# A two-layer decoder kernel: both heads of a pair step together in the attention of both layers, layer 0's memory rows of w_o are used whole, and x's first tiles and squares move at the start

## The chip, the cores and the metric

The program runs on one core of a Trainium2 chip. The metric is the device time of one execution in microseconds, the median of several runs. The core has a matrix engine (PE, also called TensorE), VectorE (DVE), ScalarE (ACT), GpSimd (POOL) and SyncE (SP), which issues most of the DMAs. Each engine works through its own instructions in order and waits on semaphores for the others.

## The reference

The input x is 256 positions by 1024, the memory another 256 by 1024, all in float32. What is computed, cut to what matters here:

```
for layer in (0, 1):
    if layer == 1: shared_kv = moba_kv(h)              # keys and values of 12 heads, once
    h = h + 0.5 * swiglu(rms_norm(h, ffn1_g[layer]))   # "a" in layer 0, "c" in layer 1
    hn = rms_norm(h, mix_g[layer])
    if layer == 0:
        u = hn @ a_w_in;  q_mem = u[..., 2 * CONV_CH:]
        primary = silu(layer_norm(conv31(a * sigmoid(gate)) + bias))   # causal, depthwise, 768 channels
    else:
        u = hn @ b_w_in;  q_mem = u[..., 768:]
        primary = causal_attention(rope(rms_norm(q)), shared_kv)       # 12 heads of 64, own block of 256
    logits = einsum('bshd,bmhd->bhsm', q_mem, k_mem)                   # 4 heads of 64, 256 memory rows
    mem_out = softmax(logits) @ v_mem
    h = h + concatenate([primary, mem_out]) @ w_o[layer]               # 768 + 256 rows
    h = h + 0.5 * swiglu(rms_norm(h, ffn2_g[layer]))   # "b" in layer 0, "d" in layer 1
```

## The kernel before

Activations stand transposed: 128 of the 1024 model channels on the partitions, the 256 positions along the free axis, so a tile of x is one of eight 128x256 pieces, k = 0 to 7. All weights are streamed from memory by SP in chunks of 1 MB (tile "raw", three buffers). Each half of a chunk is split into a high part wh, rounded by ACT (L174), and a low part wl = raw - wh, subtracted by DVE (L176). A product takes three matmuls of reduced-precision floats, high by high, high by low and low by high (function mm3); the scheduler shows them as `oao<-cat,wh` (two) and `oao<-cat,wl` (one). The activations are split the same way into y or cat (index 0 high, 1 low). Where a matmul takes plain float32 operands instead, the profile shows it as two records.

Attention (attend_pair, L469 to L537) handles a pair of heads, which share one 128-partition tile of q and k, head 0 on partitions 0 to 63 and head 1 on 64 to 127. It gives one generator for each head, with eight steps: the scores S; the row minima nb (the scores are negated) on DVE; the exponentials on ACT, with the row sums; reciprocal and scaling on DVE; the transposes of the probabilities into pp on PE; the copy pT of pp to SBUF, by ACT for head 0 and by DVE for head 1; the product with v into o; and, once for both heads, the split of o into cat by ACT and DVE. In a causal head the mask is added by an extra bfloat16 matmul of 128 columns behind each of the two score matmuls. `go(head, n)` runs the next n steps of a generator, and so the order of the calls sets the order on each engine. In layer 1 ("ab0" to "ab5" are the causal pairs, "am10" and "am11" the memory pairs) a loop over the 16 heads does, for head h: scaling and transposes of h, scores of h+2, exponentials of h+2 and so on; the row "order" PVA makes PE, DVE and ACT keep to that order.

In layer 0 the convolution has 31 taps for 768 channels. Five of its six channel groups are done by PE and DVE; parts of them and of the last go as multiply on ACT (cq, L712) and add on POOL (L713), the last group's POOL chain being the longest. Then come the layer norm over channels (mean lnm, subtraction, squares L766, sums lnv, the variance lnvc, the power lnr on POOL, its broadcast lnb), Silu, and the split into cat. The memory attention of layer 0 ("am00", "am01") runs beside it. The output projection ("oao" in layer 0, "obo" in layer 1) starts with the memory rows k = 6 and 7, whose cat comes first, and then takes k = 0 to 5 for each of the eight output tiles m. In layer 0 the low parts of the first four halves of w_o are subtracted by POOL (L180), each behind a POOL instruction named in `lo_after`.

At the start raw0's first quarter is the first DMA on SP, and x's tiles come on the ACT and SP queues. The squares of x are made by ACT and summed by seven adds on POOL (L258) into aacc, from which the first RMS norm comes (anrp on PE).

Of the kernel before, what the change touches and what calls it, by code (L numbers as in the profile page):

```python
# [17 lines left out]
P = 128  # L18
DM = 1024
KD = DM // P  # L20
SEQ = 256
# [27 lines left out]
LO_POOL = 4  # L49
TURN_AT = 3  # L50
# [28 lines left out]
def tile_kernel(ctx: ExitStack, tc: tile.TileContext, w, xT, memT, pos, vec, hg, const, out):  # L79
# [43 lines left out]
    state = {"chunk": 0, "half": 0, "raw": None, "order": "", "last": {}}  # L123
# [40 lines left out]
    def half_chunk(lo_after=None):  # L164
# [7 lines left out]
        for c in range(0, HC, q):  # L172
            s = slice(c, c + q)
            state["act"] = nc.scalar.activation(wh[:, s], raw[:, s], AF.Copy)  # L174
            if lo_after is None:
                state["dve"] = nc.vector.tensor_tensor(wl[:, s], raw[:, s], wh[:, s].bitcast(F32), op=ALU.subtract)  # L176
        if lo_after is None:
            pass
        else:
            behind(nc.gpsimd.tensor_tensor(wl, raw, wh.bitcast(F32), op=ALU.subtract), lo_after)  # L180
# [3 lines left out]
    def tiles_of(n_half, n_lo=0, lo_after=None):  # L184
        for n in range(n_half):
            wh, wl = half_chunk(lo_after[n] if n < n_lo else None)
            for i in range(8):
                yield wh[:, i * P:(i + 1) * P], wl[:, i * P:(i + 1) * P]
# [109 lines left out]
    def ffn(name, y, acc, nexts, store=False, both=False, hook=None, after=None):  # L298
# [3 lines left out]
        for j in range(KF):  # L302
# [4 lines left out]
            if first and j == 0:  # L307
# [161 lines left out]
    def attend_pair(name, qT, kT, v, vcol0, pair, cat, kc, causal, third=-1):  # L469

        po = {}

        def steps(e):
            hs = slice(e * HD, (e + 1) * HD)
            S = psum(f"{name}s{e}", *(("mm", 4) if e == third else ("sc", 2)))
            if causal:
                spans = ((0, P), (P, 3 * P))
                width = 3 * P
            else:
                spans = ((0, SEQ), (SEQ, 2 * SEQ))  # L480
                width = 2 * SEQ
            for t, (lo, hi) in enumerate(spans):
                mmul(S[:, lo:hi], qT[hs, pair, t * P:(t + 1) * P], kT[hs, pair, :hi - lo],
                     start=True, stop=not causal)
                if causal:
                    mmul(S[:, hi - P:hi], identb, maskb, start=False, stop=True)
            yield

            nb = tp.tile([P, NT], F32, name=f"{name}n{e}", tag="nb", bufs=4)
            if causal:  # L490
                for t, (lo, hi) in enumerate(spans):
                    in_order("V", nc.vector.tensor_reduce(nb[:, t:t + 1], S[:, lo:hi], axis=AX.X, op=ALU.min))
            else:
                in_order("V", nc.vector.tensor_reduce(nb, S.rearrange("p (t k) -> p t k", t=NT), axis=AX.X,
                                                      op=ALU.min))
            yield
            pr = tp.tile([P, 512], F32, name=f"{name}p{e}", tag="pr", bufs=4)
            sm = tp.tile([P, NT], F32, name=f"{name}u{e}", tag="sm", bufs=4)
            for t, (lo, hi) in enumerate(spans):
                state["func"] = in_order("A", nc.scalar.activation(  # L500
                    pr[:, lo:hi], S[:, lo:hi], AF.Exp, bias=nb[:, t:t + 1], scale=-1.0, accum_out=sm[:, t:t + 1]))
            yield
            rs = tp.tile([P, NT], F32, name=f"{name}rs{e}", tag="rs", bufs=4)
            in_order("V", nc.vector.reciprocal(rs, sm))
            for t, (lo, hi) in enumerate(spans):
                in_order("V", nc.vector.tensor_scalar(pr[:, lo:hi], pr[:, lo:hi], rs[:, t:t + 1], None, op0=ALU.mult))
            yield
            pp = psum(f"{name}pp{e}", "aux", 2)
            if causal:
                blocks = ((0, 0), (P, P), (2 * P, 2 * P))  # L510
            else:
                blocks = ((0, 0), (P, 2 * P), (2 * P, P), (3 * P, 3 * P))
            for src, dst in blocks:
                transp(pp[:, dst:dst + P], pr[:, src:src + P], ident)
            yield
            pT = tp.tile([P, 512], F32, name=f"{name}t{e}", tag="pT")
            if e:
                in_order("V", nc.vector.tensor_copy(pT[:, :width], pp[:, :width]))
            else:
                in_order("A", nc.scalar.activation(pT[:, :width], pp[:, :width], AF.Copy))  # L520
            yield
            if e == 0:
                po[0] = psum(name + "o")
            o = po[0]
            vc = slice(vcol0 + e * HD, vcol0 + (e + 1) * HD)
            mmul(o[hs, :SEQ], v[:, 0, vc], pT[:, :SEQ], start=True, stop=False)
            if causal:
                mmul(o[hs, P:SEQ], v[:, 1, vc], pT[:, SEQ:SEQ + P], start=False, stop=True)
            else:
                mmul(o[hs, :SEQ], v[:, 1, vc], pT[:, SEQ:], start=False, stop=True)  # L530
            yield
            if e:
# [456 lines left out]
```

## Time and profile before

| | us |
|---|---|
| median of 3 runs | 1023.68 |
| the runs lie between | 1020.43 and 1024.15 |
| the profiled execution | 1020.23 |
| its span, first to last instruction | 1018.1 |
| PE busy | 1000.8 (98%), 5828 matmuls |
| DVE busy | 749.1 (74%) |
| ACT busy | 592.7 (58%) |
| POOL busy | 151.7 (15%) |

The mean granted clock of PE is 0.993 of full speed. A row of the timeline names the start in us from the span's beginning, the length, the engine, the line, the instruction, output and inputs, the shapes, the number of records merged, and in brackets how long the engine had been idle and what released it. An x4 of a plain float32 product is two matmuls. The ends of matmuls are modelled, so the time that one takes from the others is read from the start of one row to the start of the next.

### The profile page before, as it was taken

Reading aid. Unit: us, or ns where it says so; the run is one execution under the profiler, and the core shown is the slowest. Engines: PE = TensorE matmul, PEld = TensorE weight load, DVE = VectorE, ACT = ScalarE, POOL = GpSimd, SP = SyncE. Lnnn points to the kernel's source line nnn. Section 1 sums busy time; section 2 is a strip of 40 time slices with the busy share of each in tenths; the row PEclk is TensorE's granted clock in tenths of the full one; section 3 lists DMA queues with packets and bytes.
Section 4 is the critical chain, followed back from the end, with each engine's and each line's share of the span. In section 5 each row is a group of like instructions: output and inputs, shape, how many; then the busy total and the mean of one; then the engine's idle time right before and its main releaser. Section 6 shows DMA issues by size and latency. Waiting matters only on the chain.

```text
span 1018.1 us, 15614 instructions
## 1 busy us (share of the span) xinstructions
PE 1000.8 (98%) x5828; PEld 868.4 (85%) x5828; DVE 749.1 (74%) x1332; ACT 592.7 (58%) x1117; POOL 151.7 (15%) x164
## 2 busy tenths in 40 slices
PE   8999999999899999999999999999999999999998
PEld 6888888898679888888888888888995798888887
DVE  7987776769867877767766877767786488777663
ACT  6787665547556655555556765555554465555542
POOL 3310000148812000001131020001150030000000
PEclk9999999999989999999999999999999999999999
DMA  8656455534134655554545455546441046545560
GB/s 302 224 196 207 173 200 182 192 103 146 42 108 146 221 188 201 174 204 171 201 165 205 169 186 187 194 179 205 170 163 42 1 166 207 201 171 202 171 227 22
DMA packets 26427, 173.44 MB, mean 170 GB/s; under 512 B 3184, under 2 KB 4592, under 8 KB 6000
## 3 DMA queue, kind: packets, MB, share of 16 engines
q1 hardware_dynamic: 25776, 171.76, 48.1%
q8 instruction: 45, 0.74, 0.3%
q10 hardware_dynamic: 576, 0.70, 0.2%
q14 instruction: 30, 0.25, 0.1%
HBM read 171.39 MB, written 1.05 MB: 169 GB/s over the span
## 4 chain that ended last, share of the span: by engine, by line
PE 92%; DVE 3%; ACT 2%; POOL 1%; DMA 1%; issue 1%; SPq 0%; DVEq 0%; POOLq 0%; ACTq 0%
PE cg L143 8%; PE dg L143 6%; PE du L143 6%; PE co L143 6%; PE ao L143 6%; PE do L143 6%; PE bo L143 6%; PE bg L143 6%; PE bu L143 6%; PE ag L143 6%; PE au L143 6%; PE cu L143 6%; PE kv L143 3%; PE oao L143 2%; PE mkv L143 2%; PE obo L143 2%
## 5 line engine op out<-in xcount | busy, mean ns | idle before, releaser
L176 DVE TENSOR_TENSOR wl<-raw,wh 128x1024 fp32r<-128x1024 f32 (+1 forms) x309 | 380.1, 1231 | 178.4 <-ACT wh L174 177.8
L174 ACT ACTIVATE wh<-raw 128x1024 fp32r<-128x1024 f32 (+1 forms) x313 | 330.2, 1057 | 303.3 <-PE dg L143 28.4
L143 PE MATMUL ag<-y,wh 128*128 128x512 f32 x176 | 63.6, 396 | 1.8 <-DVE y L249 1.8
L143 PE MATMUL dg<-oby,wh 128*128 128x512 f32 x176 | 63.6, 400 | 0.0
L143 PE MATMUL cg<-by,wh 128*128 128x512 f32 x176 | 62.7, 395 | 0.8 <-DVE cgs L216 0.8
L143 PE MATMUL au<-y,wh 128*128 128x512 f32 x176 | 63.5, 396 | 0.0
L143 PE MATMUL du<-oby,wh 128*128 128x512 f32 x176 | 63.4, 399 | 0.0
L143 PE MATMUL cu<-by,wh 128*128 128x512 f32 x176 | 62.7, 395 | 0.0
L143 PE MATMUL bg<-oay,wh 128*128 128x512 f32 x176 | 62.4, 395 | 0.0
L143 PE MATMUL bu<-oay,wh 128*128 128x512 f32 x176 | 62.2, 394 | 0.0
L143 PE MATMUL co<-chs,wh 128*128 128x512 f32 (+1 forms) x198 | 61.9, 369 | 0.0
L143 PE MATMUL ao<-ahs,wh 128*128 128x512 f32 (+1 forms) x198 | 61.9, 369 | 0.0
L143 PE MATMUL do<-dhs,wh 128*128 128x512 f32 (+1 forms) x198 | 61.9, 369 | 0.0
L143 PE MATMUL bo<-bhs,wh 128*128 128x512 f32 (+1 forms) x198 | 61.9, 368 | 0.0
L143 PE MATMUL ag<-y,wl 128*128 128x256 f32 x176 | 49.9, 284 | 0.3 <-DVE wl L176 0.3
L143 PE MATMUL ao<-ahs,wl 128*128 128x256 f32 x176 | 49.7, 283 | 0.0
L143 PE MATMUL co<-chs,wl 128*128 128x256 f32 x176 | 49.7, 283 | 0.0
L143 PE MATMUL cu<-by,wl 128*128 128x256 f32 x176 | 49.6, 282 | 0.0
L143 PE MATMUL do<-dhs,wl 128*128 128x256 f32 x176 | 49.6, 283 | 0.0
L143 PE MATMUL bo<-bhs,wl 128*128 128x256 f32 x176 | 49.6, 283 | 0.0
L143 PE MATMUL au<-y,wl 128*128 128x256 f32 x176 | 49.5, 282 | 0.0
L143 PE MATMUL cg<-by,wl 128*128 128x256 f32 x176 | 49.4, 281 | 0.0
(983 smaller groups left out, 2519.8 us busy)
## 6 DMA issues: line engine op xcount, KB each, us to landing
raw<-in_w SPq DMA_DIRECT2D x158, 1024.0 KB, 4.8
raw<-in_w SPq DMA_DIRECT2D x5, 512.0 KB, 7.3
mT<-in_memT SPq DMA_DIRECT2D x1, 1024.0 KB, 8.4
out<-x SPq DMA_DIRECT2D x8, 128.0 KB, 2.0
raw<-in_w SPq DMA_DIRECT2D x2, 256.0 KB, 4.2
x<-in_xT ACTq DMA_DIRECT2D x2, 256.0 KB, 5.5
x<-in_xT SPq DMA_DIRECT2D x2, 256.0 KB, 4.8
gt<-in_hg SPq DMA_DIRECT2D x1, 192.0 KB, 4.5
```

Source lines behind the costliest of these rows:

```text
L143: return in_order("P", nc.tensor.matmul(*a, **k))
L174: state["act"] = nc.scalar.activation(wh[:, s], raw[:, s], AF.Copy)
L176: state["dve"] = nc.vector.tensor_tensor(wl[:, s], raw[:, s], wh[:, s].bitcast(F32), op=ALU.subtract)
```

## The change

Four things are changed. Both heads of a pair now go through attend_pair in one generator, and each step does both heads: the score matmuls alternate between head 0 and head 1, as do those with v; one mask matmul of 2x128 columns serves both spans of a head; in causal pairs both copies pT are made by ACT. The loop of layer 1 goes over eight pairs: scale p, scores and minima of p+2, exponentials of p+1, the product with v of p-1, transposes and copies of p.

In layer 0 the memory attention's result is kept whole in float32 (`whole`), and the memory rows of w_o are taken from raw unsplit, two matmul records for each of 16 products instead of three matmuls. POOL subtracts no low parts any more. The rest of w_o is packed so that k = 0 to 3 of all eight m come first, then k = 4 and 5 for each m. Its first four halves are split by ACT and DVE, and `hold` puts these behind the last square and the last mean subtraction of the layer norm. In the convolution's first chunks, the mean of squares stands before the gate's last product, and the broadcast and first gated output stand behind the third product rather than the eighth.

At the start x's first two tiles come first on SP, the others sooner, and the sum of squares is one DVE reduction over eight square tiles in place of seven POOL adds.

```
-LO_POOL = 4
-TURN_AT = 3
+TURN_AT = 2
...
+    nc.sync.dma_start(x[:, :2], xT[:, :2])
     nc.sync.dma_start(raw0[:, :HC // 2], w[0][:, :HC // 2])
-    nc.scalar.dma_start(x[:, :2], xT[:, :2])
+    nc.scalar.dma_start(x[:, 4:6], xT[:, 4:6])
     nc.sync.dma_start(x[:, 2:4], xT[:, 2:4])
     nc.sync.dma_start(raw0[:, HC // 2:HC], w[0][:, HC // 2:HC])
-    nc.scalar.dma_start(x[:, 4:6], xT[:, 4:6])
+    nc.scalar.dma_start(x[:, 6:], xT[:, 6:])
     nc.sync.dma_start(raw0[:, HC:], w[0][:, HC:])
-    nc.sync.dma_start(x[:, 6:], xT[:, 6:])
...
+            state["dve"] = nc.vector.tensor_tensor(wl[:, s], raw[:, s], wh[:, s].bitcast(F32), op=ALU.subtract)
+            if state["hold"]:
+                for i, other in zip((state["act"], state["dve"]), state["hold"]):
+                    behind(i, other)
...
+                sq = cp.tile([P, KD, SEQ], F32, name="sq0", tag="kv")
                 for k in range(KD):
-                    square_sum(f"{name}q0{k}", acc, x[:, k], k == 0)
+                    nc.scalar.activation(sq[:, k], x[:, k], AF.Square)
+                nc.vector.tensor_reduce(acc, sq.rearrange("p k s -> p s k"), axis=AX.X, op=ALU.add)
...
+    def attend_pair(name, qT, kT, v, vcol0, pair, causal, tag, done):
+        hs = [slice(e * HD, (e + 1) * HD) for e in range(2)]
+        S = [psum(f"{name}s{e}", *(("mm", 4) if tag == "mm" else ("sc", 2))) for e in range(2)]
+        spans = ((0, P), (P, 3 * P)) if causal else ((0, SEQ), (SEQ, 2 * SEQ))
+        width = spans[1][1]
+        opened = []
+        for t, (lo, hi) in enumerate(spans):
+            for e in range(2):
+                i = mmul(S[e][:, lo:hi], qT[hs[e], pair, t * P:(t + 1) * P], kT[hs[e], pair, :hi - lo],
+                         start=t == 0 or not causal, stop=not causal, skip_group_check=causal)
+                if t:
+                    behind(i, opened[e])
+                opened.append(i)
+        if causal:
+            for e in range(2):
+                mmul(S[e].rearrange("p (a b) -> p a b", b=2 * P)[:, :, :P], identb,
+                     maskb[:, None, :].to_broadcast([P, 2, P]), start=False, stop=True, skip_group_check=True)
+        yield
...
+        pT = [tp.tile([P, 512], F32, name=f"{name}t{e}", tag="pT") for e in range(2)]
+        in_order("A", nc.scalar.activation(pT[0][:, :width], pp[0][:, :width], AF.Copy))
+        if causal:
+            in_order("A", nc.scalar.activation(pT[1][:, :width], pp[1][:, :width], AF.Copy))
+        else:
+            in_order("V", nc.vector.tensor_copy(pT[1][:, :width], pp[1][:, :width]))
+        yield
+        o = psum(name + "o")
+        vc = [slice(vcol0 + e * HD, vcol0 + (e + 1) * HD) for e in range(2)]
+        for e in range(2):
+            mmul(o[hs[e], :SEQ], v[:, 0, vc[e]], pT[e][:, :SEQ], start=True, stop=False)
+        for e in range(2):
...
+        yield
+        done(o[:, :SEQ])
+        yield
...
+    def to_whole(dst, i):
+        def done(o):
+            state["func"] = in_order("A", nc.scalar.activation(dst[:, i], o, AF.Copy))
+        return done
...
+            start = m % 2 == 0 and k == CC
+            if k >= CC and whole is not None:
+                c = ((k - CC) * KD + m) * P
+                i = mmul(o[m], raw[:, c:c + P], whole[:, k - CC], start=start, stop=False, skip_group_check=True)
+            else:
+                i = mm3(o[m], next(it), cat, k, start, last, skip_group_check=True)
...
+        early = CC - 2 if whole is not None else 0
+        state["hold"] = hold
+        for k in range(early):
+            for m in range(KD):
+                mm(m, k, False)
+        state["hold"] = None
         for m in range(KD):
-            for k in range(CC):
+            for k in range(early, CC):
...
+    whole = hc[:, CC * (PAD + SEQ):CC * (PAD + SEQ) + 2 * SEQ].rearrange("p (i s) -> p i s", i=2)
...
+            mm3(pa[:, :SEQ], wts[0][KD - 1], y[0], KD - 1, False, True)
             v = mean_cols("cnr", acc)
+            mm3(pg[:, :SEQ], wts[1][KD - 1], y[0], KD - 1, False, True)
...
-            mm_group(pa, y[0])
-            rr["b"] = bcast_rows("cnb", rr["r"])
-            glu_out(0, *rr["p"])
+            for k, wt in enumerate(tiles_of(1)):
+                mm3(pa[:, :SEQ], wt, y[0], k, k == 0, k == KD - 1)
+                if k == 2:
+                    rr["b"] = bcast_rows("cnb", rr["r"])
+                    glu_out(0, *rr["p"])
...
+    oproj = out_proj("oa", cat, V_FFN2, whole, (hi, lo))
+    go(pairs[0], 2)
+    go(pairs[1], 4)
+    go(pairs[0], 2)
+    pv = psum("lnv", "mm", 4)
...
     tables(AF.Silu)
+    go(pairs[1], 2)
     with tc.high_priority():
         rlb = bcast_rows("lnb", rl)
-    next(oproj)
-    next(oproj)
+    go(pairs[1], 2)
+    for _ in range(5):
+        next(oproj)
...
+    go(pairs[0], 3)
...
+    n = len(pairs)
+    for p in range(n + 1):
+        if p < n:
+            go(pairs[p], 1)
+        if p == TURN_AT:
             for turn in turns:
                 turn()
+        if p + 2 < n:
+            go(pairs[p + 2], 2)
+        if p + 1 < n:
+            go(pairs[p + 1], 1)
+        if p:
+            go(pairs[p - 1], 2)
+        if p < n:
+            go(pairs[p], 2)
+        if p >= n - 2:
             next(oproj)
...
+        rest = [t[:, :, :early].transpose(0, 2, 1, 3).reshape(P, -1), t[:, :, early:CC].reshape(P, -1)]
+        chunks(np_.concatenate(rest, axis=1))
...
-    out_w(d["w_o"][0])
+    out_w(d["w_o"][0], CC - 2)```

PE in the loop of layer 1, ahead of the scores of the pair ab4; S tiles are ab4s, o tiles ab2o or ab1o, transposed probabilities pp. Before:

```order
L143 MATMUL ab4s_8239<-kvs,q1T 128x128
L143 LDWEIGHTS identb
L143 MATMUL ab4s_8239<-maskb,identb 128x128
L143 MATMUL ab4s_8239<-kvs,q1T 128x256
L143 LDWEIGHTS identb
L143 MATMUL ab4s_8239<-maskb,identb 128x128
L143 MATMUL ab2o<-ab2t_8233,kvs 64x256
L143 MATMUL ab2o<-ab2t_8233,kvs 64x128
L146 MATMUL ab3pp_8255<-cst,ab3p_8210 128x128 x3
```

The nine rows are the work of one head and come twice for a pair. The same place on PE now, where 8143 and 8144 are the S tiles of the two heads:

```order
L142 MATMUL ab4s_8143<-kvs,q1T 128x128
L142 MATMUL ab4s_8144<-kvs,q1T 128x128
L142 MATMUL ab4s_8143<-kvs,q1T 128x256
L142 MATMUL ab4s_8144<-kvs,q1T 128x256
L142 LDWEIGHTS identb
L142 MATMUL ab4s_8143<-maskb,identb 128x2x128
L142 LDWEIGHTS identb
L142 MATMUL ab4s_8144<-maskb,identb 128x2x128
L142 MATMUL ab1o<-ab1t_8131,kvs 64x256
L142 MATMUL ab1o<-ab1t_8132,kvs 64x256
L142 MATMUL ab1o<-ab1t_8131,kvs 64x128
L142 MATMUL ab1o<-ab1t_8132,kvs 64x128
```

Six transposes of ab2 follow. The work of both heads stands side by side, and the product with v is that of the pair before the one whose transposes follow.

ACT in layer 0, from the squares of the layer norm (hc<-hc) to the first Silu (lp), with the second memory pair's exponentials am01p between. Before:

```order
L766 ACTIVATE hc<-hc 128x256 x6
L500 ACTIVATE am01p_2936,am01u_2937<-am01s_2931,am01n_2934 128x256 x2
L500 ACTIVATE am01p_2959,am01u_2960<-am01s_2954,am01n_2957 128x256 x2
L533 ACTIVATE cat_2836<-am00o 128x256
L140 ACT_TABLE_LOAD
L140 ACTIVATE warm<-onec 128x1
L520 ACTIVATE am01t_2992<-am01pp_2987 128x512
L803 ACTIVATE lp_3036<-lz_3034,vt 128x256
```

And now the same stretch:

```order
L799 ACTIVATE hc<-hc 128x256 x6
L173 ACTIVATE wh_0_3062<-raw_3060 128x1024
L173 ACTIVATE wh_1_3090<-raw_3060 128x1024
L173 ACTIVATE wh_0_3120<-raw_3118 128x1024
L173 ACTIVATE wh_1_3148<-raw_3118 128x1024
L504 ACTIVATE am01p_2935,am01u_2937<-am01s_2925,am01n_2931 128x256 x2
L552 ACTIVATE hc<-am00o 128x256
L139 ACT_TABLE_LOAD
L139 ACTIVATE warm<-onec 128x1
L504 ACT_TABLE_LOAD
L504 ACTIVATE am01p_2936,am01u_2938<-am01s_2926,am01n_2932 128x256 x2
L525 ACTIVATE am01t_2985<-am01pp_2975 128x512
```

A third table load and the first Silu follow. Four high parts have come between the squares and the exponentials, and the table is changed three times where it was changed once. On DVE, the first rows behind the minima am01n, up to the layer norm's variance lnvc and the scaling am01p; now:

```order
L497 TENSOR_REDUCE am01n_2932<-am01s_2926 128x2
L174 TENSOR_TENSOR wl_0_3063<-raw_3060,wh_0_3062 128x1024
L174 TENSOR_TENSOR wl_1_3091<-raw_3060,wh_1_3090 128x1024
L174 TENSOR_TENSOR wl_0_3121<-raw_3118,wh_0_3120 128x1024
L174 TENSOR_TENSOR wl_1_3149<-raw_3118,wh_1_3148 128x1024
L812 TENSOR_SCALAR lnvc<-lnv 128x2
```

These four low parts stood on POOL before; they are now ahead of lnvc on DVE.

## Rows read from the trace of the kernel before

**Rows 1.** The page: chain that ended last by engine, and two costly groups.

```profile
PE 92%; DVE 3%; ACT 2%; POOL 1%; DMA 1%; issue 1%; SPq 0%; DVEq 0%; POOLq 0%; ACTq 0%
L176 DVE TENSOR_TENSOR wl<-raw,wh 128x1024 fp32r<-128x1024 f32 (+1 forms) x309 | 380.1, 1231 | 178.4 <-ACT wh L174 177.8
L174 ACT ACTIVATE wh<-raw 128x1024 fp32r<-128x1024 f32 (+1 forms) x313 | 330.2, 1057 | 303.3 <-PE dg L143 28.4
```

**Rows 2.** Windows: stretch, its length, PE, PEld, DVE, ACT, POOL busy, clock, DMA.

```profile
778.61:789.16 10.55, 10.55 (x54) 6.22 (x53) 6.79 (x25) 5.19 (x22) 0.00 (x0) 1.00 0.00 1
...
295.70:299.00 3.30, 3.30 (x18) 3.30 (x17) 1.90 (x3) 2.33 (x5) 0.00 (x0) 0.51 0.00 0
9.00:12.50 3.50, 3.50 (x13) 2.91 (x12) 3.50 (x5) 3.01 (x7) 3.27 (x4) 0.51 0.96 358
```

**Rows 3.** Timeline, PE, from one head of layer 1's loop.

```profile
789.16 0.49 PE L143 MATMUL ab4s<-kvs,q1T 64*128 64x128 f32 x2
...
790.36 0.23 PE L143 MATMUL ab4s<-maskb,identb 128*128 128x128 bf16 x1
790.52 0.86 PE L143 MATMUL ab2o<-ab2t,kvs 128*64 128x256 f32 x4
791.32 0.55 PE L146 MATMUL ab3pp<-cst,ab3p 128*128 128x128 f32 x3
```

**Rows 4.** Timeline, PE: two heads in one stretch, and one head alone.

```profile
291.67 1.09 PE L143 MATMUL am01o<-am01t,mv 128*64 128x256 f32 x8
752.74 1.14 PE L143 MATMUL am10s<-mk,q1T 64*128 64x256 f32 x8
760.19 1.13 PE L143 MATMUL am11s<-mk,q1T 64*128 64x256 f32 x4
```

**Rows 5.** Timeline, ACT: one copy of transposed probabilities in the loop.

```profile
791.96 0.49 ACT L520 ACTIVATE ab3t<-ab3pp 128x384 f32<-128x384 f32 x1 [0.15 <-PE ab3pp L146]
```

**Rows 6.** Timeline, PE: memory pairs and the projection behind the loop.

```profile
767.81 1.08 PE L143 MATMUL am10o<-am10t,mv 128*64 128x256 f32 x4 [0.98 <-DVE am10t L518]
...
799.97 0.40 PE L143 MATMUL obo<-cat,wh 128*128 128x256 f32 x2
...
800.33 0.40 PE L143 MATMUL obo<-cat,wh 128*128 128x256 f32 x2
```

**Rows 7.** Line L713 (POOL's adds of the convolution): idle before it.

```profile
  ACT cq L712: 9.6, 5
```

**Rows 8.** Timeline, layer 0's layer norm and memory attention, all engines.

```profile
273.65 0.62 DVE L506 TENSOR_SCALAR am00p<-am00p,am00rs 128x256 f32<-128x256 f32 x2
...
274.81 7.06 POOL L180 TENSOR_TENSOR wl<-raw,wh 128x1024 fp32r<-128x1024 f32 x3
...
275.36 2.07 PE L143 MATMUL lnm<-hc,onem 128*128 128x256 f32 x4 [4.84 <-DVE hc L724]
275.42 4.24 DVE L506 TENSOR_SCALAR am00p<-am00p,am00rs 128x256 f32<-128x256 f32 x2
...
282.79 2.71 PE L143 MATMUL lnv<-onel,hc 128*128 128x1 f32 x23
...
283.75 0.68 DVE L494 TENSOR_REDUCE am01n<-am01s 128x2 f32<-128x512 f32 x1
...
287.78 1.28 ACT L140 ACT_TABLE_LOAD   x1
...
289.08 0.20 ACT L140 ACTIVATE warm<-onec 128x1 f32<-128x1 f32 x1
...
294.64 0.51 PE L143 MATMUL oao<-cat,wh 128*128 128x256 f32 x2 [1.88 <-DVE cat L534]
```

**Rows 9.** Timeline, the start: first product, a square, a later product.

```profile
8.08 0.50 PE L143 MATMUL ag<-y,wh 128*128 128x512 f32 x1 [1.83 <-DVE y L249]
...
8.66 0.41 ACT L257 ACTIVATE aq<-x 128x256 f32<-128x256 f32 x1
...
13.92 0.39 PE L143 MATMUL ag<-y,wl 128*128 128x256 f32 x1 [0.28 <-DVE wl L176]
```

More of the change, by code (lines that the diff above doesn't have):

```diff
@@ L120, in tile_kernel @@
     nc.vector.memset(mhalf, -0.5)
-    state = {"chunk": 0, "half": 0, "raw": None, "order": "", "last": {}}
+    state = {"chunk": 0, "half": 0, "raw": None, "order": "", "last": {}, "hold": None}
     def behind(i, other):
@@ L467, in queries @@
         return use
[L469 to L489, printed above, removed]
+    def attend_pair(name, qT, kT, v, vcol0, pair, causal, tag, done):
[16 more added lines that the diff above has]
+        yield
+        nb = [tp.tile([P, NT], F32, name=f"{name}n{e}", tag="nb", bufs=4) for e in range(2)]
+        for e in range(2):
@@ L513, in steps @@
[L513 to L524, printed above, removed]
@@ L553, in mem_kv, with out_proj @@
         return kT, v
-    def out_proj(name, cat, g, *lo):
+    def out_proj(name, cat, g, whole=None, hold=None):
         o = []
-        it = tiles_of(KD, *lo)
-        first = {}
+        raw = raw_chunk() if whole is not None else None
+        it = tiles_of(KD if whole is None else KD - 2)
         def mm(m, k, last):
-            i = mm3(o[m], next(it), cat, k, m % 2 == 0 and k == CC, last, skip_group_check=True)
+            start = m % 2 == 0 and k == CC
+            if k >= CC and whole is not None:
+                c = ((k - CC) * KD + m) * P
+                i = mmul(o[m], raw[:, c:c + P], whole[:, k - CC], start=start, stop=False, skip_group_check=True)
+            else:
+                i = mm3(o[m], next(it), cat, k, start, last, skip_group_check=True)
             if k == CC:
-                first[m] = i
                 if m % 2:
-                    behind(i, first[m - 1])
+                    behind(i, state["first"])
+                else:
+                    state["first"] = i
         for m in range(0, KD, 2):
@@ L575, in out_proj @@
             mm(m + 1, CC, False)
+        if whole is not None:
+            yield
         for m in range(KD):
@@ L743, in tile_kernel @@
     cat = y_tiles("cat0")
-    heads = [st for pr_ in range(2)
-             for st in attend_pair(f"am0{pr_}", qT, kT, v, pr_ * P, pr_, cat, CC + pr_, False)]
+    pairs = [attend_pair(f"am0{i}", qT, kT, v, i * P, i, False, "sc", to_whole(whole, i)) for i in range(2)]
     last_conv(22)
@@ L751, in tile_kernel @@
         nc.vector.tensor_tensor(cv[:, CC - 1], last[:, :SEQ], cv[:, CC - 1], op=ALU.add)
-    go(heads[0], 4)
-    go(heads[1], 4)
+    go(pairs[0], 4)
     pm = psum("lnm", "aux", 2)
@@ L805, in tile_kernel @@
         nc.vector.tensor_tensor(cat[:, c, 1], p_, cat[:, c, 0].bitcast(F32), op=ALU.subtract)
-    go(heads[2], 2)
-    go(heads[3], 2)
-    next(oproj)
     state["order"] = ""
@@ L835, in tile_kernel @@
     mq = qT[:, NPAIR:]
[L836 to L842 removed]
+    pairs = [attend_pair(f"am1{i}", mq, kT, v, i * P, i, False, "mm" if i % 2 else "sc", to_cat(cat, CC + i))
+             for i in range(2)]
+    pairs += [attend_pair(f"ab{i}", qT, kTs, vs, i * P, i, True, "mm" if i % 2 else "sc", to_cat(cat, i))
+              for i in range(NPAIR)]
     proj("mq1", y, queries("mq1", re, G_MQ + 1, qT, NPAIR, False, nc.gpsimd))
```

125 lines of the change are left out of this document (43 added, 82 removed).

## The prediction, made before the changed kernel ran

> **What bounds the kernel now.** I read the chain of waits first: 92% of it is PE, with DVE, ACT and POOL at 3% or less each [rows 1]. So a term counts only where PE idles, or where PE's own time shrinks. The windows come next, to see what PE does in the two attention stretches. In the loop of layer 1, 10.55 us for two pairs, PE is busy all the time while DVE is busy 6.79 and ACT 5.19 [rows 2]: PE alone sets the pace there, 5.27 a pair. Then the timeline of one head of that loop, for what PE spends on what [rows 3], and of the few places where two heads' matmuls stand side by side [rows 4]. Last the layer norm of layer 0, where PE does wait: 4.84 us before lnm and 1.88 before oao [rows 8], and the start, where it waits 1.83 [rows 9].
>
> **Layer 1, the loop.** A head before: from the scores at 789.16 to the product with v at 790.52 are 1.36, the two masks in it 790.52 - 790.36 = 0.16 each, so the scores alone are 1.04. The product with v takes 791.32 - 790.52 = 0.80, and the rest of the head's 10.55 / 4 = 2.64, 0.47, is the three transposes [rows 2, 3].
>
> What side by side is worth is in the trace already: eight score records of two heads took 1.14, four of one head 1.13; eight records of products with v took 1.09, four 256 wide in am10o 1.08 [rows 4, 6]. The second head's cost nothing there: each head has 64 of the 128 rows (form 64*128) or columns (128*64). So a pair's scores cost 1.04 and its products with v 0.80. The transposes fill the whole array and stay at 2 x 0.47 = 0.94. A mask of 256 columns has no row; it lies between 0.16 (one mask of 128) and 0.32 (two); I take 0.21, near the lower, since it is the row of the same instruction, so 0.42 for two. Sum 1.04 + 0.42 + 0.80 + 0.94 = 3.20.
>
> The others must keep up. DVE loses one copy of transposed probabilities a pair, which I price like ACT's, 0.49 [rows 5]: 6.79 / 2 - 0.49 = 2.9. ACT gains it: 5.19 / 2 + 0.49 = 3.1 [rows 2, 5]. Both are under 3.20, with little to spare: 0.1 on ACT. In the new order ACT's queue has the exponentials of p+1, then the split of p-1, then the copies of p, and PE has the scores of p+2 to do while the copies run, so no engine waits for the other within a turn unless ACT slips. Six causal pairs save 6 x (5.27 - 3.20) = 12.4. In the two memory pairs the scores of am11 and the products with v of both go side by side; am10's scores already did. At 1.05 for each of the three [rows 4, 6] that is 3.1.
>
> Against it stand new waits at the head of the loop. One wait is there now, 0.98 before am10o [rows 6]. With both heads in one step, PE has less to do while DVE scales two heads, so the first pairs wait longer: between nothing and one turn of DVE, 2.9. I take 1.5. Layer 1: -12.4 - 3.1 + 1.5 = -14.0. Bounds: -15.5 without new waits; with a period of 4.0 in place of 3.20, -9.2.
>
> **Layer 0.** The path to lnm is POOL's chain of adds, which waited 9.6 us in five places for ACT's cq [rows 7]. Now the gated output that opens the chain comes five products sooner: 5 x 0.36 (800.33 - 799.97, [rows 6]) = 1.8. And the high parts of w_o no longer stand among the cq's on ACT; they were two pairs of 1.06 [rows 1]. I take 2.9 of the rest of those waits as gone. Together -4.7, between 0 and -9.6.
>
> Behind lnm, DVE's scaling of am00p took 4.24 beside POOL's subtractions and 0.62 before they began [rows 8]. The mean is copied by DVE behind it, at 275.42 + 4.24 = 279.66, while lnm had ended at 275.36 + 2.07 = 277.43. With no low parts on POOL that 2.2 goes. The wait before oao (1.88) goes too, because PE now has the whole product of k = 0 to 3 behind k = 6 and 7.
>
> What comes in: four high parts on ACT behind the last square and four low parts on DVE behind the first of these, 1.06 + 4 x 1.23 = 6.0 [rows 1], ahead of lnvc on DVE. The sums of squares on PE cover some 2.8 of it (2.71, [rows 8]), which leaves +3.2. This is the cost of the hold: on POOL these subtractions stood beside the path. Then two more table loads on ACT, of 1.28 each [rows 8], one ahead of the second head's exponentials and one ahead of the first Silu. The second is hidden while oao runs, since k = 6 and 7 need no Silu; the first is not: +1.3.
>
> The Trainium skill (ScalarE: Activation LUTs, What ACT_TABLE_LOAD costs) adds about 1.38 us of draining to a load's 1.28. Here the load at 287.78 ends at 289.06 and the next ACT row starts at 289.08 [rows 8], so the trace shows no such drain; by the page both loads together would cost 2.8 more, and the sum would be 1006.9.
>
> Last, the 16 memory products are two plain float32 records each, in place of three matmuls at 0.36. Nothing in the rows shows that record alone with 128 rows; from am01o and am10o, four records of 256 columns in 1.08 [rows 6], it is 0.27 or less, so a product at most 0.54 and at least the 0.36 of the old one. I take the middle, 0.45: 16 x 0.09 = +1.4, between 0 and +2.9. Layer 0: -4.7 - 2.2 - 1.9 + 3.2 + 1.3 + 1.4 = -2.9. Between everything hidden, -6, and nothing gained before lnm, +1.5.
>
> **The start.** ACT has five more squares and one more y ahead of the second quarter of wh, 6 x 0.41 = 2.5, and DVE's one reduction of 2048 elements a partition, at 0.68 for 512 [rows 8, 9], is 2.7, ahead of the second wl: 5.2 of work put before what PE needs for its second k. At most 1.8 of it comes back by x landing first (PE's wait before its first product, [rows 9]). So the product that stood at 13.92 moves by between -1.8 and 5.2 - 1.8 = +3.4. I take the middle, +0.8. The seven POOL adds cost PE nothing before: no row of PE waits for them.
>
> **The sum.** Against the profiled execution's 1020.2: 1020.2 - 14.0 - 2.9 + 0.8 = 1004.1. The median of the runs shown is 3.5 above that execution; I put a quarter of this on top: 1005.
>
> **The rivals.**
>
> ACT becomes the bound of the loop. PE and ACT are 0.1 apart, and each turn has several handovers between them, any of which may open a gap; a period of 4.0 adds 6 x 0.8 = 4.8, so 1009 to 1010. For it: the copies are the last thing in ACT's turn, and both the next transposes and the next product with v wait for them. Against it: PE has scores queued in just that gap. The Trainium skill (TensorEngine Tiling (Array Packing), PSUM Bottleneck) says that side-by-side tiles speed TensorE but not the emptying of PSUM, which may then be the bound. By that rule the pair's time would be ACT's 3.1 or more, which is what this rival prices. No row of before bears on it, as PE set the pace.
>
> Layer 0 and the start lose. If POOL's chain ends no earlier, or the held halves stay whole on the path, layer 0 gives +1.5; with +2.5 at the start the sum is 1020.2 - 14.0 + 4.0 = 1010. For it: the hold puts 6.0 of splitting on the path that POOL used to hide.
>
> Layer 0 gives all its bound, -6: 1020.2 - 14.0 - 6 + 0.8 = 1001, 1002 beside the median.
>
> The heads don't run side by side once they are causal, with scores 128 and 256 wide in one accumulation. Then a pair saves only the masks, 4 x 0.16 - 0.42 = 0.2, and the sum is 1020.2 - 1.3 - 2.9 + 0.8, about 1017. Against it: memory scores did so in the same form [rows 4].
>
> On the other side: the clock. PE's granted clock was at the lower of its two levels (1.2 GHz of 2.4), 0.51 in the rows' scale, from 9.0 to 12.5 behind the idle time of 1.83, and again from 295.7 to 299 behind 1.88 [rows 2, 8, 9]; the 0.98 before am10o cost nothing of it, as the loop ran at 1.00 [rows 2, 6]. If new waits of two us and more come at the head of the loop, and gaps in each turn keep it low, PE's 3.20 becomes 6.4. It decides from the share of the loop at the low level: at 65% a pair takes 5.27 again. In the whole loop it is 6 x 1.1 = +6.8 and, with the memory pairs likewise, about +10: 1020.2 + 10 - 2.9 + 0.8 = 1028, and 1029 beside the median. Against it: PE would still be busy nearly all the time, as 3.20 of work a turn leaves no idle time.
>
> **How the numbers follow.** Chances: my forecast 0.61, with its own range of 1000.5 to 1009; ACT as the bound 0.15; layer 0 and the start losing 0.12; all of layer 0's bound 0.05; heads not side by side 0.03; the low clock 0.04. The range must reach both 1010s and some way past, and down to layer 0's bound with no new waits: 999.5 to 1012. A measurement of this kernel tells some 0.5%, about 5 us, from no change. From the median that puts the limit at 1018.6; the first four cases are all below it. Heads apart and half of the low clock lie within 0.5%, the rest is slower; with something for what I have not thought of, 0.93, 0.04 and 0.03.
>
> **What would show it.** The loop right: the scores of ab3, ab4 and ab5 start 3.2 to 3.4 us apart, and obo ends some 14 us sooner against the first memory scores. Wrong: 4 us apart, with PE waiting for ACT's copies. Layer 0 right: lnm without a wait, low parts on DVE between the squares and lnvc, no wait between k = 6 and k = 3 of oao. Wrong: idle time of PE before am01o or lnb. The start right: a wait of PE for the reduction at about 13 us and the next k within 1 us of before. My prediction is wrong as a whole if the six causal pairs together save less than 8 us.

## The result, and the profile after

The changed kernel took 1012.15 us (median; 1011.14 to 1012.63), beside 1022.94 for the kernel before on the same chip: a ratio of 0.9896, 95% interval 0.9875 to 0.9918. It is faster by 10.8 us, where 18 were forecast, and lies just above the range's upper end of 1012. Its profiled execution took 1012.62 us, with a span of 1010.5.

Four landmarks split the difference, each the first matmul of a stage: mkv, the products with the memory's keys and values; bo, the last product of layer 0's second feed-forward part (part b); am10s, layer 1's first memory scores; and dg, the last feed-forward part. The timeline's summary by tile gives form, count, shortest, median and longest duration in ns, and the first and last start in us. Of the kernel before:

```profile
L143 PE MATMUL mkv<-wh,my x64: 387/389/403, 61.4 to 599.6; 128*128 128x512 f32 x64
L143 PE MATMUL bo<-bhs,wh x198: 274/396/400, 439.9 to 501.5; 128*128 128x512 f32 x154, 128*128 128x256 f32 x44
L143 PE MATMUL am10s<-mk,q1T x8: 376/376/480, 752.7 to 753.5; 64*128 64x256 f32 x8
L143 PE MATMUL dg<-oby,wh x176: 387/398/476, 827.5 to 949.3; 128*128 128x512 f32 x176
```

And of the changed kernel:

```profile
L142 PE MATMUL mkv<-wh,my x64: 389/389/395, 66.1 to 606.2; 128*128 128x512 f32 x64
L142 PE MATMUL bo<-bhs,wh x198: 279/396/398, 446.5 to 508.2; 128*128 128x512 f32 x154, 128*128 128x256 f32 x44
L142 PE MATMUL am10s<-mk,q1T x8: 376/376/480, 759.3 to 760.1; 64*128 64x256 f32 x8
L142 PE MATMUL dg<-oby,wh x176: 387/398/476, 819.9 to 941.7; 128*128 128x512 f32 x176
```

At mkv, behind the start, the changed kernel is 4.7 us late. At bo, behind layer 0's mixer and most of its second feed-forward part, it is 6.6 late. From am10s to dg, which is layer 1's attention and output projection, it goes from 6.6 late to 7.6 early: 14.2 gained, where 14.0 were forecast.

The 1.9 us lost between mkv and bo are not all the change's doing. The products of part b ran at two paces in the two traced executions, at a granted clock of 1.00 in both. Eight of them (x16, each a matmul with wh and one with wl) take, in the chain that ended last, before and after:

```profile
345.78 2.77 PE bg L143 x16
```

```profile
339.25 2.83 PE bg L142 x16
```

Over the part's 352 products that makes some 2.3 us, as the last section shows. Without it layer 0 gained 0.4, where 2.9 were forecast. So the start is worse than forecast, layer 0 gained little, and 2.3 us lie in a part whose code wasn't changed.

The loop of layer 1 in the changed kernel, PE's timeline, to be held against [rows 3]:

```profile
781.66 0.93 PE L142 MATMUL ab3s<-kvs,q1T 64*128 64x128 f32 x8
782.51 0.39 PE L142 MATMUL ab3s<-maskb,identb 128*128 128x256 bf16 x2
782.84 0.87 PE L142 MATMUL ab0o<-ab0t,kvs 128*64 128x256 f32 x8
783.64 0.87 PE L145 MATMUL ab1pp<-cst,ab1p 128*128 128x128 f32 x6
784.44 0.93 PE L142 MATMUL ab4s<-kvs,q1T 64*128 64x128 f32 x8
```

A pair takes 784.44 - 781.66 = 2.78 us, against 5.27 [rows 2] and a forecast of 3.20: scores 0.85, masks 0.33, products with v 0.80, transposes 0.80. The window over two pairs, with the columns of [rows 2], shows that ACT is now as full as PE, 5.52 of 5.57:

```profile
781.66:787.23 5.57, 5.57 (x50) 3.52 (x49) 5.32 (x23) 5.52 (x23) 0.00 (x0) 1.00 0.01 1
```

The start, all engines, against [rows 9]:

```profile
6.34 0.50 PE L142 MATMUL ag<-y,wh 128*128 128x512 f32 x1
...
10.38 3.73 DVE L317 TENSOR_REDUCE aacc<-sq 128x256 f32<-128x2048 f32 x1
10.92 0.50 PE L142 MATMUL ag<-y,wh 128*128 128x512 f32 x1 [2.60 <-ACT wh L173]
...
14.16 1.01 PE L142 MATMUL anrp<-onec,aacc 128*128 128x1 f32 x4 [2.05 <-DVE aacc L317]
...
17.74 0.41 PE L142 MATMUL ag<-y,wl 128*128 128x256 f32 x1
```

PE begins at 6.34 rather than 8.08, then waits 2.60 for the second quarter of wh, which stands behind all eight squares, and 2.05 for the reduction. The product that stood at 13.92 now stands at 17.74.

Layer 0, against [rows 8]:

```profile
272.90 2.88 PE L142 MATMUL lnm<-hc,onem 128*128 128x256 f32 x12
...
285.93 1.28 ACT L139 ACT_TABLE_LOAD   x1
286.73 0.16 DVE L812 TENSOR_SCALAR lnvc<-lnv 128x2 f32<-128x2 f32 x1
...
287.44 1.28 ACT L504 ACT_TABLE_LOAD   x1
288.73 0.47 ACT L504 ACTIVATE am01p<-am01s,am01n 128x256 f32<-128x256 f32 x1
...
290.35 1.94 PE L145 MATMUL am01pp<-cst,am01p 128*128 128x128 f32 x8 [4.56 <-DVE am01p L512]
292.86 2.17 PE L142 MATMUL am01o<-am01t,mv 128*64 128x256 f32 x8
```

The wait before lnm's last products is gone, but there is a new one of 4.56 before am01pp: two table loads stand on ACT between the exponentials of one head and those of the other. PE runs at the lower of its two clock levels there; am01o took 2.17 for what took 1.09 in [rows 4]. The windows show both stretches of low clock:

```profile
14.00:20.00 6.00, 5.84 (x21) 5.26 (x22) 5.31 (x7) 1.53 (x2) 2.75 (x1) 0.50 0.61 205
284.00:296.00 12.00, 7.44 (x37) 5.76 (x38) 6.43 (x16) 9.13 (x19) 0.71 (x1) 0.59 0.45 175
```

### The profile page after: what moved, and what is told of

Same layout as the page of the kernel before. It is cut to its first block, busy times and chain, and to the rows that moved or that the text cites. A ratio compares the mean times of both kernels' runs of the same rounds, so it can differ in the third digit from the quotient of the medians.

```text
span 1010.5 us, 15551 instructions
## 1 busy us (share of the span) xinstructions
PE 989.4 (98%) x5800; PEld 860.6 (85%) x5800; DVE 742.4 (73%) x1327; ACT 596.7 (59%) x1123; POOL 136.0 (13%) x153
## 3 DMA queue, kind: packets, MB, share of 16 engines
HBM read 171.39 MB, written 1.05 MB: 171 GB/s over the span
## 4 chain that ended last, share of the span: by engine, by line
PE 88%; ACT 3%; DVE 3%; POOL 3%; issue 1%; DMA 1%; ACTq 0%; DVEq 0%; POOLq 0%
PE cg L142 6%; PE dg L142 6%; PE du L142 6%; PE bu L142 6%; PE bg L142 6%; PE co L142 6%; PE ao L142 6%; PE do L142 6%; PE bo L142 6%; PE ag L142 6%; PE au L142 6%; PE cu L142 6%; PE kv L142 3%; POOL hc L748 3%; PE obo L142 2%; PE mkv L142 2%
## 5 line engine op out<-in xcount | busy, mean ns | idle before, releaser
L174 DVE TENSOR_TENSOR wl<-raw,wh 128x1024 fp32r<-128x1024 f32 (+1 forms) x311 | 382.1, 1231 | 192.2 <-ACT wh L173 191.3
L173 ACT ACTIVATE wh<-raw 128x1024 fp32r<-128x1024 f32 (+1 forms) x311 | 328.6, 1058 | 316.6 <-PE dg L142 28.4
L142 PE MATMUL ag<-y,wh 128*128 128x512 f32 x176 | 64.2, 400 | 2.6 <-ACT wh L173 2.6
L142 PE MATMUL au<-y,wh 128*128 128x512 f32 x176 | 63.7, 397 | 0.0
L142 PE MATMUL bu<-oay,wh 128*128 128x512 f32 x176 | 63.7, 400 | 0.0
L142 PE MATMUL dg<-oby,wh 128*128 128x512 f32 x176 | 63.6, 400 | 0.0
L142 PE MATMUL bg<-oay,wh 128*128 128x512 f32 x176 | 63.6, 399 | 0.0
L142 PE MATMUL cg<-by,wh 128*128 128x512 f32 x176 | 62.7, 395 | 0.8 <-DVE cgs L213 0.8
L142 PE MATMUL du<-oby,wh 128*128 128x512 f32 x176 | 63.4, 399 | 0.0
L142 PE MATMUL cu<-by,wh 128*128 128x512 f32 x176 | 62.7, 395 | 0.0
L142 PE MATMUL ao<-ahs,wh 128*128 128x512 f32 (+1 forms) x198 | 61.9, 369 | 0.0
L142 PE MATMUL co<-chs,wh 128*128 128x512 f32 (+1 forms) x198 | 61.9, 369 | 0.0
L142 PE MATMUL bo<-bhs,wh 128*128 128x512 f32 (+1 forms) x198 | 61.9, 369 | 0.0
L142 PE MATMUL do<-dhs,wh 128*128 128x512 f32 (+1 forms) x198 | 61.9, 369 | 0.0
L142 PE MATMUL bg<-oay,wl 128*128 128x256 f32 x176 | 49.5, 281 | 0.7 <-DVE wl L174 0.7
L142 PE MATMUL ag<-y,wl 128*128 128x256 f32 x176 | 50.1, 285 | 0.0
L142 PE MATMUL au<-y,wl 128*128 128x256 f32 x176 | 49.9, 284 | 0.0
L142 PE MATMUL co<-chs,wl 128*128 128x256 f32 x176 | 49.7, 283 | 0.0
L142 PE MATMUL ao<-ahs,wl 128*128 128x256 f32 x176 | 49.7, 283 | 0.0
L142 PE MATMUL cu<-by,wl 128*128 128x256 f32 x176 | 49.6, 282 | 0.0
L142 PE MATMUL bo<-bhs,wl 128*128 128x256 f32 x176 | 49.6, 283 | 0.0
L142 PE MATMUL do<-dhs,wl 128*128 128x256 f32 x176 | 49.6, 283 | 0.0
```

Source lines behind the costliest of these rows:

```text
L142: return in_order("P", nc.tensor.matmul(*a, **k))
```

## The experiments

My theory was that the three parts add, and that the start and layer 0 each lose by a cause of its own, a queue order at the start and two table loads in layer 0. The time of a run is the median of four executions, with their range behind it. The kernel before was run again beside them, with medians from 1020.11 to 1022.84, so a difference of 1 or 2 us between two medians tells little. Where it matters I also read the landmarks in the one traced execution of each kernel. There part b alone differs by 2.3 us, as in the result.

**Layer 1 alone (l1_only).** The kernel before, with the new loop in layer 1 only:

```diff
-    go(heads[0], 4)
-    go(heads[1], 4)
+    go(pairs[0], 3)
...
+    n = len(pairs)
+    for p in range(n + 1):
```

> The kernel before with the new attend_pair and loop in layer 1 alone; layer 0 and the start as before. If layer 1 gave 14.2 us in the changed kernel by itself, between the first scores of am10 and the first product of the last feed-forward part, this gives the median of before, 1020 to 1023, less 14.2: 1006 to 1009. Rival: part of that gain comes from the layers ahead of it, by weights that are loaded sooner: 1010 or more.

1008.82 (1007.74 to 1009.17), ratio 0.987 (0.9847 to 0.9894). The theory held: layer 1 gives all of the gain, and by the medians some 3 us more than the whole change. In its trace am10s to dg takes 61.8 against 74.8 before, 13.0 gained; PE's clock was at 0.50 there for 3.4 us, from 768.7, and at 1.00 in the changed kernel's loop, which gained 14.2.

**Do the heads have to alternate? (serial)** The changed kernel, with the two loops exchanged for the scores, and likewise for the products with v:

```diff
-        for t, (lo, hi) in enumerate(spans):
-            for e in range(2):
+        for e in range(2):
+            for t, (lo, hi) in enumerate(spans):
```

> The changed kernel with the two heads of a pair one behind the other again inside a step, on PE alone: both scores of head 0, then both of head 1, and the same with the products with v. If PE runs two heads at once only when their matmuls alternate in its queue, a pair loses up to 1.0 + 0.8 us, six causal pairs 11 and the memory pairs 4: 1020 to 1027. Rival: it is enough that they stand next to each other, as the eight score records of am10 in the kernel before did, where two of one head came before two of the other: 1012, within 1 us of the changed kernel.

1011.0 (1009.03 to 1012.2). The rival held: no loss. PE's timeline of this kernel shows the same pair:

```profile
781.37 0.93 PE L142 MATMUL ab4s<-kvs,q1T 64*128 64x128 f32 x8
782.24 0.39 PE L142 MATMUL ab4s<-maskb,identb 128*128 128x256 bf16 x2
782.56 0.88 PE L142 MATMUL ab1o<-ab1t,kvs 128*64 128x256 f32 x8
783.37 0.88 PE L145 MATMUL ab2pp<-cst,ab2p 128*128 128x128 f32 x6
784.17 0.93 PE L142 MATMUL ab5s<-kvs,q1T 64*128 64x128 f32 x8
```

A pair takes 2.80. The order of the two heads within a step doesn't matter; it is enough that their products stand next to each other.

**The start as before (start_old).** DMAs and squares both undone:

```diff
+    nc.sync.dma_start(raw0[:, :HC // 2], w[0][:, :HC // 2])
+    nc.scalar.dma_start(x[:, :2], xT[:, :2])
...
-                    nc.scalar.activation(sq[:, k], x[:, k], AF.Square)
-                nc.vector.tensor_reduce(acc, sq.rearrange("p k s -> p s k"), axis=AX.X, op=ALU.add)
+                    square_sum(f"{name}q0{k}", acc, x[:, k], k == 0)
```

> The start is as in the kernel before (x's DMAs and the seven POOL adds), the rest as changed. The start's loss, 4.7 us at the first product with the memory's keys and values (61.33 before, 65.98 changed), is thought to stay to the end: 1012.15 - 4.7 = 1007.5. Rival: later waits absorb it, since layer 0's POOL chain or the weight stream sets the time there: 1011 to 1012.

1008.01 (1004.13 to 1008.86): 4.1 us back, and mkv starts at 61.4 again in the traced execution, which was the fastest. The loss at the start stays to the end.

**The new order of the DMAs alone (start_dma).** Only the squares undone:

```diff
-                nc.vector.tensor_reduce(acc, sq.rearrange("p k s -> p s k"), axis=AX.X, op=ALU.add)
+                    square_sum(f"{name}q0{k}", acc, x[:, k], k == 0)
```

> Only the squares go back to seven POOL adds; x's DMAs stay in the new order. If the squares ahead of the second quarter of wh and the one reduction ahead of its wl are the whole loss, this gives 1006 to 1007.5, with PE's first product at 6.3 and no wait for aacc. Rival: the order of the DMAs brings part of the loss, by putting more y tiles ahead of the second wh on ACT: 1009 to 1010.

1012.25 (1009.47 to 1013.22): nothing back. Here the theory fell: the order of the DMAs costs by itself nearly as much as with the squares. In the traces mkv starts at 65.0, against 66.1 in the changed kernel and 61.4 before, so the order alone brings 3.6 of the 4.7; the 1.1 that came back was lost again in layer 1, where am10s to dg took 62.2 rather than 60.6. The timeline of the start says how:

```profile
8.96 0.50 PE L142 MATMUL ag<-y,wh 128*128 128x512 f32 x1 [1.22 <-ACT wh L173]
9.13 3.08 DVE L246 SCALAR_TENSOR_TENSOR y<-x,vt,y 128x256 fp32r<-128x256 f32 x4
9.36 4.57 POOL L255 TENSOR_TENSOR aacc<-aacc,aq 128x256 f32<-128x256 f32 x5 [0.30 <-ACT aq L254]
...
13.40 0.58 PE L142 MATMUL ag<-y,wl 128*128 128x256 f32 x1 [3.23 <-DVE wl L174]
```

With x there early, the low parts of the last y tiles go ahead of the second wl on DVE, four of them in 3.08 beside POOL's adds, where they took 1.67 in the changed kernel with POOL idle. PE waits 3.23 for that wl.

**The squares held back (sq_held).** The changed kernel, with squares and reduction behind the split of raw0's second half:

```diff
+                    if k == 2:
+                        held = state["act"], state["dve"]
...
+                    behind(nc.scalar.activation(sq[:, k], x[:, k], AF.Square), held[0])
+                behind(nc.vector.tensor_reduce(acc, sq.rearrange("p k s -> p s k"), axis=AX.X, op=ALU.add), held[1])
```

> The eight squares are held behind the high part of raw0's second half and the one reduction behind its low part; everything else as changed. If the place of the reduction in the queues is what costs, and not its length, the start loses no more than 1 us: 1007 to 1008.5, with anrp no longer a wait of PE. Rival: the length of the reduction, 3.7 us on DVE, delays later low parts as much wherever it stands: 1010.5 or more.

1008.74 (1006.73 to 1010.91): most of it back, with mkv at 63.3. Place matters, but the reduction, 3.81 here, still held PE up by 1.70 before anrp. So both readings had a part.

**Silu's table behind the exponentials (table).** The changed kernel with one dependency moved:

```diff
     go(pairs[1], 4)
+    exps = state["func"]
     go(pairs[0], 2)
+    state["func"] = exps
```

> The load of Silu's table in layer 0 stands behind the last exponentials of the second memory pair and no longer behind the copy of am00o; everything else as changed. If two of the three table loads are on the path of PE's wait of 4.6 before am01pp, they go and with them 2.9 us, and a little more by the clock: 1008.5 to 1009.5. Rival: lnvc, the power and its broadcast, which end only little earlier, are next on that path: 1011 or more.

1008.79 (1007.19 to 1009.63): 3.4 us back. The wait before am01pp fell from 4.56 to 2.5, and mkv to bo takes 377.6 in the trace against 380.4 in the changed kernel, with part b at the same pace in both. So 2.8 of the 3.4 lie in layer 0, and that the two loads cost about that much is shown.

**Both losses undone (old_table).** The old start and the moved table load in one kernel:

```diff
+    nc.scalar.dma_start(x[:, :2], xT[:, :2])
...
+                    square_sum(f"{name}q0{k}", acc, x[:, k], k == 0)
...
+    state["func"] = exps
```

> The start as in the kernel before, and Silu's table in layer 0 loaded behind the last exponentials; the rest as changed. If the two losses are apart, they add: 1008.0 less 3 to 3.4 is 1004.6 to 1005, which is what was predicted for the changed kernel. Rival: behind a shorter start layer 0's path is another, the power and broadcast of the layer norm: 1006.5 or more.

1003.1 (1002.41 to 1003.58), ratio 0.9815 (0.9792 to 0.9839). The losses add, and 1.5 us more is gained than their sum: 4.1 + 3.4 off 1012.15 would be 1004.6. The traced execution has part b at its faster pace, like that of the kernel before, so the two can be compared between mkv and bo:

```profile
L142 PE MATMUL mkv<-wh,my x64: 387/389/398, 61.5 to 596.2; 128*128 128x512 f32 x64
L142 PE MATMUL bo<-bhs,wh x198: 281/396/400, 436.9 to 498.7; 128*128 128x512 f32 x154, 128*128 128x256 f32 x44
```

That is 375.4 against 378.5 before: layer 0 gains 3.1 here. This is 9 us faster than the changed kernel and the fastest version that was run, though 2.3 of the 9 are the pace of part b in the traced executions.

**Without hold (old_table_nohold).** The same, with the first four halves of w_o split whenever their data is there:

```diff
-    oproj = out_proj("oa", cat, V_FFN2, whole, (hi, lo))
+    oproj = out_proj("oa", cat, V_FFN2, whole)
```

> As old_table, without holding the first four halves of w_o's split behind the layer norm's squares and subtractions. The four high parts stand among the products cq again and the low parts on DVE beside the convolution. If hold's price ahead of lnvc, 2.7 us, and its gain in POOL's chain, 2.9, are both real, this stays within 1 us of old_table. Rival: hold only costs: 2.5 us below old_table.

1006.6 (1006.37 to 1008.54): 3.5 slower by the medians, which neither expectation has. But the traces don't put this on hold. From mkv to bo it takes 378.1 against 375.4, and 2.3 of these 2.7 are part b at its slower pace. What is left, 0.4, agrees with the first expectation, that hold's price and its gain about cancel. The waits show both: the 2.5 before am01pp are gone, and POOL's chain ends late again, so that PE waits before lnm as it did in [rows 8]:

```profile
276.98 2.08 PE L142 MATMUL lnm<-hc,onem 128*128 128x256 f32 x4 [4.41 <-DVE hc L756]
```

**The reduction with the old DMAs (sq_only).** As old_table, but with eight squares and one reduction:

```diff
-                    square_sum(f"{name}q0{k}", acc, x[:, k], k == 0)
+                    nc.scalar.activation(sq[:, k], x[:, k], AF.Square)
+                nc.vector.tensor_reduce(acc, sq.rearrange("p k s -> p s k"), axis=AX.X, op=ALU.add)
```

> As old_table (x's DMAs in the old order, Silu's table behind the exponentials), but with the eight squares and the one reduction on VectorE. With the old order of the DMAs the second quarter of wh stands behind four squares rather than eight and its wl ahead of the reduction, so if the squares cost by their place in the queues only, and the new DMA order is what puts them there: within 1 us of old_table's 1003.1. Rival: the reduction costs by its length, 3.7 us on VectorE ahead of the second chunk's low parts: 1005.5 to 1007.

1006.65 (1005.6 to 1007.07): 3.5 slower than with POOL's adds. The rival held. In the traces mkv starts at 63.6 against 61.5, so 2.1 of it is shown to lie at the start. PE waits 1.05 for the sum and 0.53 for the low part behind it; the reduction took 3.83:

```profile
12.36 3.83 DVE L317 TENSOR_REDUCE aacc<-sq 128x256 f32<-128x2048 f32 x1
...
16.24 0.61 PE L142 MATMUL anrp<-onec,aacc 128*128 128x1 f32 x4 [1.05 <-DVE aacc L317]
17.38 0.39 PE L142 MATMUL ag<-y,wl 128*128 128x256 f32 x1 [0.53 <-DVE wl L174]
```

**The same, held back (old_table_sqheld).** As sq_only, with squares and reduction behind the split:

```diff
...
+                    behind(nc.scalar.activation(sq[:, k], x[:, k], AF.Square), held[0])
+                behind(nc.vector.tensor_reduce(acc, sq.rearrange("p k s -> p s k"), axis=AX.X, op=ALU.add), held[1])
```

> As sq_only, with squares and reduction held behind the split of raw0's second half. If what PE waits for at the start is the second quarter of wh and wl, this brings both forward by the squares' time and gains some of the 1.9 us that PE waited there: 1001.5 to 1003. Rival: the reduction of 3.7 us in front of the next chunk's low part makes up for it: 1004 or more.

1005.98 (1005.42 to 1008.63): not distinguishable from sq_only, 2.9 above old_table. No place that was tried makes the reduction pay.

**The first scaling of layer 1 sooner (old_table_scale).** As old_table, with one more step of am10 ahead of the last query product:

```diff
-    go(pairs[0], 3)
+    go(pairs[0], 4)
...
-        if p < n:
+        if 0 < p < n:
             go(pairs[p], 1)
```

> As old_table, with the scaling of the first memory pair am10 in layer 1 ahead of the last query product and not behind it. If the waits of PE at the head of the loop, 1.3 and 0.6 us before am10pp, come from this scaling standing late on VectorE, they go: 1001 to 1002. Rival: the wait for the last queries (before the scores of ab2) grows by as much: 1003.

1003.91 (1003.37 to 1004.92): no gain. Of the waits at the head of the loop, the 1.3 went, 0.9 before ab2s stayed, and new ones of 0.6 before am10o and 0.5 before am10pp came. In the traces am10s to dg takes 60.1 rather than 61.9, but old_table's clock was at 0.50 there from 763.7 to 767.1, and part b ran at its slower pace here. So whether the edit itself gains anything is not shown.

## Why the prediction was wrong

The mechanism and the main term were right: the second head's half-array products cost nothing beside the first's, and layer 1, put at -14.0, gave -14.2. That it came so close is partly luck. A pair takes 2.78, not 3.20, since scores, masks and transposes were dearer in my count than they are, and six pairs at that period would have saved 6 x 2.49 = 14.9 rather than 12.4. New waits at the head of the loop came out as allowed: 1.34, 0.64 and 0.95 against 0.26, 0.98 and 0.26 before, 1.4 more where I took 1.5. What I had at nothing are places where PE's products took longer than in the loop. The scores of ab2, behind such a wait, took 779.51 - 778.39 = 1.12 rather than 0.85, and at the end the products with v are cut in two by the output projection, so that ab4o takes 0.58 + 0.80 rather than 0.80:

```profile
795.00 0.65 PE L142 MATMUL ab4o<-ab4t,kvs 128*64 128x256 f32 x2
795.58 0.38 PE L142 MATMUL obo<-cat,wh 128*128 128x256 f32 x1
...
796.01 0.86 PE L142 MATMUL ab4o<-ab4t,kvs 128*64 128x256 f32 x6
```

The rival of ACT as the bound came near: ACT is 99% busy in the loop, but at a shorter period than PE's forecast one.

**The start is the first step that failed.** It was put at +0.8 between -1.8 and +3.4. The product that stood at 13.92 moved by 3.8 to 17.74, and mkv by 4.7, both outside these bounds. The +0.8 is the middle: it takes half of the squares and the reduction as hidden, without a reason, and nothing of them was hidden. The squares put the second quarter of wh 2.5 later on ACT, as forecast (10.25 rather than 7.74), and x's earlier landing gave back 1.74 of that, so that PE's first product with it comes 0.86 later. Then the reduction stands in front of the second wl. It was priced at 2.7, from 0.68 for 512 neighbouring elements; over eight tiles, with neighbours 256 apart, it takes 3.73. PE's first product with that wl starts at 15.04 rather than 11.76, 3.3 later. The rest is the clock, which the sum left out here: at 0.51 from 13.1 to 20.0, where a stretch half as long stands in [rows 2]. Nor would x's landing have helped without the reduction: the new order of the DMAs alone moves mkv by 3.6 (start_dma).

**Layer 0 is the second.** It was put at -2.9, and without part b's pace it gave -0.4. Up to lnm it did better than forecast: lnm's last product ends 209.7 behind mkv, against 216.0 before, 6.3 sooner where I took 4.7, a part of it by the clock, which stood at 0.57 from 275 to 279 before. The memory products came out at 0.43 each (16 of them in 295.70 - 288.88 in old_table_nohold), against 0.45. What failed is the term of the table loads. I had one of the two extra loads hidden behind oao, at +1.3 for the other; in truth the order puts two loads between the exponentials of head 0 and head 1, as the order rows ahead of the prediction already show, and the third is the one that is hidden. From 285.93 to 288.73 that is 2.8, and moving the one load gave 2.8 back in the trace. With it layer 0 gains 3.1, about the forecast, though that still has the wait of 2.5 before am01pp. The price of the hold, put at +3.2, isn't shown apart from what it gains in POOL's chain; together they come to a gain of 0.4 in the traces.

The profiled execution took 8.5 more than the sum's 1004.1. These two steps make 3.9 + 2.5 of it. Another 2.3 is the pace of part b, which no term of the sum has and which the change isn't shown to cause. It is more than the 0.15 by which the measured time lies outside the range, so on which side of 1012 it fell was partly chance. Two slips in the working move nothing: with nothing gained before lnm, layer 0 is -2.9 + 4.7 = +1.8 and not +1.5, and ACT has two more y ahead of the second quarter of wh, not one.

The Trainium skill (ScalarE: Activation LUTs, What ACT_TABLE_LOAD costs) would have had a load cost 2.66 with its drain. In the changed kernel the first exponential starts at 288.73, 1.29 behind the load at 287.44, so the trace again shows no drain; the path was lengthened by the number of loads on it.

The clock rival was right in kind and wrong in place. Layer 1's loop ran at full clock in the changed kernel. Its low stretches are at the start, behind PE's wait of 2.60 and from within that of 2.05, and in layer 0, from 279.4 to 282.8 behind waits of 1.11 and 0.81 and from 286.2 to 296.4 within and behind that of 4.56. In l1_only and old_table a stretch of 3.4 us stands in layer 1 too.

## What to carry to other kernels

Where a profile has products that use half of the array, look for a place where those of two heads already stand next to each other: that one row prices the main term, and here it was right. A dependency that fixes where a function table is loaded has to name the last use of the old table, or a scheduler may put the load between two uses, as here. At a kernel's start, data that lands sooner lets less urgent work in front of the urgent in each engine's order; count what it overtakes, not only when it lands. And before a difference of some us between two kernels is put down to an edit, compare a stage that the edit doesn't touch.

## What was not expected of the hardware

PE runs the matmuls of two heads side by side also when the queue holds two of one head before two of the other: 2.80 us a pair against 2.78.

Executions differ by more than the places that were changed. The same start code had mkv at 61.4 in the kernel before and at 63.5 in l1_only. And feed-forward part b has two paces at a granted clock of 1.00. It shows in single products too, two steps from one bg product with wh to the next taking 0.69 in the kernel with the old start and 0.71 in the changed one:

```profile
340.23 0.39 PE L142 MATMUL bg<-oay,wh 128*128 128x512 f32 x1
...
340.58 0.39 PE L142 MATMUL bg<-oay,wh 128*128 128x512 f32 x1
...
340.92 0.39 PE L142 MATMUL bg<-oay,wh 128*128 128x512 f32 x1
```

```profile
339.80 0.40 PE L142 MATMUL bg<-oay,wh 128*128 128x512 f32 x1
...
340.15 0.40 PE L142 MATMUL bg<-oay,wh 128*128 128x512 f32 x1
...
340.51 0.40 PE L142 MATMUL bg<-oay,wh 128*128 128x512 f32 x1
```

From the first bg product to the first of bo that makes 124.2 and 126.5. Of the traced executions five have the slower pace (the changed kernel, start_dma, table, old_table_nohold and old_table_scale), the others the faster one. old_table_scale has old_table's code up to the end of part b and the other pace, so that code alone doesn't set it; what does stays open. The runs of one kernel differ in another way too: those of the old start, 1004.13, 1007.85, 1008.18 and 1008.86, had mean granted clocks of 0.997, 0.993, 0.991 and 0.990.
